# Block products of 256 columns: moving operand and result gone through in pieces of four columns, even pieces first

## The chip, the cores and the metric

The kernel runs on one core of one Trainium2 chip. The metric is device time in microseconds (us), the median of the runs of one program. Profiles are of one execution each. PE is TensorE's matmul, PEld its weight load, DVE VectorE, ACT ScalarE, POOL GpSimd, SP SyncE.

## What is computed

One decoder layer on 512 tokens and 16 learned meta tokens, width 2048, feed-forward width 5632, all in float32:

```python
n = rmsnorm(h, g_mix); p = n @ w_in                       # q, k, v | b, c, u
o_attn = stick_breaking_attention(rmsnorm(q), rmsnorm(k), v)   # 8 heads of 128
o_conv = b * causal_dwconv3(c * u)                        # 1024 channels
h = h + concat(rmsnorm(o_attn), rmsnorm(o_conv)) @ w_out
n2 = rmsnorm(h, g_ffn)
h = h + (silu(n2 @ w_gate) * (n2 @ w_up)) @ w_down
return h[:, N_META:]
```

## The kernel before

Activations are kept transposed: features on the 128 partitions, tokens as columns. A matmul takes a 128x128 tile of a weight matrix as the operand that is loaded into the array (LDWEIGHTS) and up to 512 token columns as the moving operand, and adds its result up in a bank of PSUM.

Every float32 operand is split into two float32r tiles, hi and lo: ACT casts (`split_quad`, L203), DVE subtracts (L206). A product of two such operands is three matmuls into the same bank: hi by hi, hi by lo, lo by hi. Each of them has its own weight load, so there are as many LDWEIGHTS as MATMULs.

The larger products go in pairs of output tiles. `pair_product` splits weights, activations and result into 2x2 blocks and forms them with seven block products where eight would be plain (weight sums `t1`, `t2`, `t3` are made by DVE, sums of activations once ahead of time). The token dimension is thus cut in halves of T2 = 256 columns. The seven block products go to three PSUM banks `y`, `z` and `x`; between them ACT copies partial results to `sides` (`read_out`, L912) and DVE combines them with later ones. After the last, ACT copies `x` out (L1267), and PE goes on with the next pair.

`block_product` does one block product: for each of n weight tiles along the contraction it issues the three matmuls of L887, L890 and L891, `act(part, k)` giving the hi or lo columns of tile k. It is used in three places:

- the convolution part (`conv_pair` with blocks of N = 258 columns, `gate_pair` with 256), whose operands are the `n` tiles and the packed `mixed` tiles;
- gate and up projections of the feed-forward part, operands `f` (44 pairs, 7 blocks, 8 tiles);
- the down projection, operands `ring` and `first` (chunks of 4, 6, 6 and 6 tiles).

Where a weight piece holds two output tiles, `ps` is 512 columns wide and is gone through in two halves of 256.

Where operands lie in SBUF is partly set by hand. `slots` puts the feed-forward operands four columns into their tile and adds a tail, and `pad` fills pools:

```python
        c = 2 * m * n * T2
        t = pool.tile([P, 4 + c + tail], dt, name=name, **kw)
        t = t[:, 4 : 4 + c].rearrange("p (s a k t) -> p s a k t", s=m, a=2, k=n)
```

The seven blocks of the convolution part come from tiles of two kinds. `raw_block` and `last_block` are columns of an `n` tile, `last_block` N = 258 columns further on than `raw_block(0, 0)`; the `mixed` blocks lie packed, 258 columns apart. `gate_pair` starts two columns further into each (`a` = 2) and takes 256:

```python
        return [
            raw_block(0, 0, a, n),
            *(mixed_block(t, a, n) for t in mixed),
            last_block(a, n),
            raw_block(1, 0, a, n),
            raw_block(1, 1, a, n),
        ]
```

The order of instructions on each engine comes from the program order and the priorities of the framework's scheduler; `keep_in_program_order` and `issue_after` pin single ones. SP's queue loads weights (`sw_in`), POOL's queue moves activations and results.

Of the kernel before, what the change touches and what calls it, by code (L numbers as in the profile page):

```python
# [26 lines left out]
T2 = SEQ // 2  # L27
# [6 lines left out]
def hybrid_layer(ctx: ExitStack, tc: tile.TileContext, xT, w_in, w_out, w_gu, w_down, vecs, out):  # L34
# [269 lines left out]
    def next_w():  # L304
        ahead = max(min(n_first, used[0] + 6), used[0] + 1 + S_AHEAD)
        if used[0] < n_first:
            ahead = min(ahead, n_first + 1)
        while len(split_w) < min(len(pieces), ahead):
            if n_first < len(split_w) <= n_first + S_AHEAD:
                with tc.issue_after(read_q0[3].ins):  # L310
                    prepare()
            else:
                prepare()
        used[0] += 1
        return split_w[used[0] - 1]
# [6 lines left out]
    def tick():  # L322
        for w in waiting:
            w[0] -= 1
        while any(w[0] <= 0 for w in waiting):
            w = next(w for w in waiting if w[0] <= 0)
            waiting.remove(w)
            w[1]()
# [156 lines left out]
    def host(m, name):  # L485
        return mpool.tile([P, 8 * N + (48 if m == 0 else 0)], F32R, tag=f"m{m}", name=name)
# [373 lines left out]
    def wide_product(parts, acts):  # L860
        hi, lo = next_w()
        for ps, a, b in parts:
            for n, (k, ah, al) in enumerate(acts):
# [4 lines left out]
                if b == SEQ:  # L868
                    tick()

    def block_product(ps, act, start):

        hi, lo = next_w()
        i = pieces[used[0] - 1][1]
        m = max(1, ps.shape[-1] // T2)
        cols = ps.shape[-1] // m  # L880
        n = pairs[i][0] // m
        for j in range(m):
            p, skip = ps[:, j * cols : (j + 1) * cols], m > 1 or not start
            for k in range(n):
                kk = slice((j * n + k) * P, (j * n + k + 1) * P)
                ah, al = act(0, k), act(1, k)
                opening = pe.matmul(p, hi[:, kk], ah, start=start and j == k == 0, stop=False, skip_group_check=skip)  # L887
                if j == k == 0:
                    tc.keep_in_program_order(opening)
                pe.matmul(p, hi[:, kk], al, start=False, stop=False, skip_group_check=skip)  # L890
                pe.matmul(p, lo[:, kk], ah, start=False, stop=k == n - 1, skip_group_check=skip)  # L891
# [8 lines left out]
    def pair_product(acts, cols, out2, side, fifth=None, hook=None):  # L900
# [16 lines left out]
        if first:  # L917
            block_product(y, acts[5], True)
            go_between()
        block_product(x, acts[0], True)  # L920
        read_out(p1, x)
        go_between()
        if hook:
            hook(1)
        block_product(z, acts[1], True)
        go_between()
        read_out(p5, z)
# [67 lines left out]
    for m in range(2):  # L995
        t = host(m, f"oa{m}")[:, : 4 * SEQ].rearrange("p (h a b) -> p h a b", h=2, a=2)
# [65 lines left out]
    for i, j in enumerate(OUT_TILES):  # L1062
# [36 lines left out]
        ps = ps_out[i]  # L1099
        half, k = divmod(j, 8)  # L1100
# [313 lines left out]
```

## Time and profile before

| what | us |
|---|---|
| median of 2 runs | 2027.59 (2027.51 to 2027.67) |
| span of the profiled execution | 2025.8 |
| attention part and its projections, up to the first block product | about 370 |
| convolution part and output projection, up to | 764 |
| feed-forward part | 764 to 2025.8 |

In rows of matmuls the form `128x256 f32` is the result's partitions and columns; `x<-f,sw_split` names the bank, the moving operand and the weights. A row of groups has count, busy time in us and mean duration in ns, then the idle time before. A row of windows has the stretch, its length, and busy time and number of instructions of each engine, then the granted clock, the share of the DMA engines and GB/s. A row of the timeline has start and duration in us.

### The profile page before, as it was taken

The numbers are of one execution on the slowest core, as the hardware profiler recorded it, in microseconds if no ns is written. First come the engines' busy times: TensorE is split into PE (matmuls) and PEld (weight loads), VectorE is DVE, ScalarE is ACT, GpSimd is POOL, SyncE is SP. The second block draws the span as 40 slices with busy tenths as digits, with TensorE's granted clock in tenths as the row PEclk, the third lists the DMA queues.
The fourth block names the chain that finished last, engine by engine and source line by source line (L and its number), as shares of the span: only waits on it lengthen the run. The fifth ranks groups of instructions, "written<-read, shape, count | busy, mean of one in ns | idle before, by whom it ended". The sixth has DMA issues, their size and how long they took to land.

```text
span 2025.8 us, 39704 instructions
## 1 busy us (share of the span) xinstructions
PE 2019.7 (100%) x16158; PEld 1961.8 (97%) x16158; DVE 1723.3 (85%) x2199; ACT 1077.9 (53%) x1559; POOL 337.3 (17%) x507
## 2 busy tenths in 40 slices
PE   9999999999999999999999999999999999999999
PEld 8999999999998889999999999999999999999999
DVE  7877777698877778999988988988988978888888
ACT  7876676444454445555555555555555544444443
POOL 0111111200014440111110110110110243131211
PEclk9999999999999999999999999999999999999999
DMA  6333343833255555556554554554554999797864
GB/s 222 116 135 115 125 136 136 282 105 110 99 198 179 165 161 194 171 153 186 173 160 148 167 164 149 164 166 151 162 166 151 290 339 352 170 318 193 222 149 91
DMA packets 156664, 356.31 MB, mean 176 GB/s; under 512 B 13696, under 2 KB 68224, under 8 KB 155712
## 3 DMA queue, kind: packets, MB, share of 16 engines
q1 hardware_dynamic: 72640, 216.73, 32.2%
q0 software_dynamic: 83696, 136.99, 25.0%
q8 instruction: 127, 2.08, 0.4%
q14 instruction: 57, 0.47, 0.1%
q10 hardware_dynamic: 144, 0.04, 0.0%
HBM read 275.78 MB, written 77.92 MB: 175 GB/s over the span
## 4 chain that ended last, share of the span: by engine, by line
PE 99%; DMA 0%; DVE 0%; SPq 0%; ACT 0%; issue 0%
PE x L887 14%; PE x L891 14%; PE x L890 14%; PE z L887 7%; PE z L890 7%; PE z L891 7%; PE y L891 3%; PE y L887 3%; PE y L890 3%; PE pk L342 3%; PE pv L342 3%; PE pq L342 3%; PE pv L340 2%; PE pk L340 2%; PE pq L340 1%; PE pb L342 1%
## 5 line engine op out<-in xcount | busy, mean ns | idle before, releaser
L203 ACT CAST sw_split<-sw_in 128x1024 fp32r<-128x1024 f32 (+3 forms) x671 | 662.4, 989 | 708.7 <-PE x L890 174.2
L206 DVE TENSOR_TENSOR sw_split<-sw_in,sw_split 128x1024 fp32r<-128x1024 f32 (+3 forms) x671 | 775.5, 1156 | 140.4 <-ACT sw_split L203 133.0
L887 PE MATMUL x<-f,sw_split 128*128 128x256 f32 x1408 | 387.5, 275 | 0.1
L891 PE MATMUL x<-f,sw_split 128*128 128x256 f32 x1408 | 387.2, 275 | 0.0
L890 PE MATMUL x<-f,sw_split 128*128 128x256 f32 x1408 | 387.2, 275 | 0.0
L887 PEld LDWEIGHTS x<-f,sw_split 128*128 128x128 f32 x1408 | 264.3, 188 | 0.7 <-DVE u L937 0.5
L890 PEld LDWEIGHTS x<-f,sw_split 128*128 128x128 f32 x1408 | 264.3, 188 | 0.0
L891 PEld LDWEIGHTS x<-f,sw_split 128*128 128x128 f32 x1408 | 264.3, 188 | 0.0
L1206 POOL DMA_DIRECT2D fd<-s x147 | 103.7, 921 | 708.0 <-DVE s L353 632.1
L887 PE MATMUL z<-f,sw_split 128*128 128x256 f32 x704 | 193.6, 275 | 0.0
L890 PE MATMUL z<-f,sw_split 128*128 128x256 f32 x704 | 193.6, 275 | 0.0
L891 PE MATMUL z<-f,sw_split 128*128 128x256 f32 x704 | 193.6, 275 | 0.0
L216 DVE TENSOR_TENSOR sw_in<-sw_in 128x1024 f32<-128x1024 f32 (+1 forms) x164 | 187.7, 1145 | 5.4 <-DMA sw_in<-w_in 0.8
L887 PE MATMUL x<-ring,sw_split 128*128 128x256 f32 x608 | 167.2, 275 | 0.0
L890 PE MATMUL x<-ring,sw_split 128*128 128x256 f32 x608 | 167.2, 275 | 0.0
L891 PE MATMUL x<-ring,sw_split 128*128 128x256 f32 x608 | 167.2, 275 | 0.0
L890 PEld LDWEIGHTS z<-f,sw_split 128*128 128x128 f32 x704 | 132.2, 188 | 0.0
L891 PEld LDWEIGHTS z<-f,sw_split 128*128 128x128 f32 x704 | 132.2, 188 | 0.0
L887 PEld LDWEIGHTS z<-f,sw_split 128*128 128x128 f32 x704 | 132.2, 188 | 0.0
L887 PEld LDWEIGHTS x<-ring,sw_split 128*128 128x128 f32 x608 | 114.1, 188 | 0.0
L891 PEld LDWEIGHTS x<-ring,sw_split 128*128 128x128 f32 x608 | 114.1, 188 | 0.0
L890 PEld LDWEIGHTS x<-ring,sw_split 128*128 128x128 f32 x608 | 114.1, 188 | 0.0
(701 smaller groups left out, 5276.9 us busy)
## 6 DMA issues: line engine op xcount, KB each, us to landing
sw_in<-w_gu SPq DMA_DIRECT2D x176, 512.0 KB, 3.8
sw_in<-w_in SPq DMA_DIRECT2D x90, 512.0 KB, 3.3
fd<-s POOLq DMA_DIRECT2D x147, 256.0 KB, 5.1
sw_in<-w_down SPq DMA_DIRECT2D x96, 384.0 KB, 4.2
ring<-fd POOLq DMA_DIRECT2D x42, 768.0 KB, 17.6
sw_in<-w_out SPq DMA_DIRECT2D x32, 512.0 KB, 3.3
out_T<-d POOLq DMA_DIRECT2D x54, 256.0 KB, 4.6
mix_dram<-st_x POOLq DMA_DIRECT2D x16, 516.0 KB, 4.1
```

The costliest lines, as they stand in the source:

```text
L203: cast[0] = sc.copy(hi, src)
L206: latest[0] = ve.tensor_tensor(lo, src, hi.bitcast(F32), ALU.subtract)
L216: return ve.tensor_tensor(sums[name], a, b, ALU.add)
L340: pe.matmul(ps, wh, ah[:, a:b], start=k + i == 0, stop=False)
L342: pe.matmul(ps, w, x[:, a:b], start=False, stop=k + i == last and x is (al if used[0] <= n_first else ah))
L887: opening = pe.matmul(p, hi[:, kk], ah, start=start and j == k == 0, stop=False, skip_group_check=skip)
L890: pe.matmul(p, hi[:, kk], al, start=False, stop=False, skip_group_check=skip)
L891: pe.matmul(p, lo[:, kk], ah, start=False, stop=k == n - 1, skip_group_check=skip)
L1206: gp.dma_start(fd[c][s][:, :, k], t[:, :, i])
```

## The change

A helper `order` rearranges a view of 256 columns: the columns are taken as 32 groups of 8, each group as two pieces of 4, and the dimension of the pieces is put first. An access through this view goes through the first pieces of all groups (columns 0 to 3, 8 to 11, 16 to 19 and so on) and then through the second pieces (4 to 7, 12 to 15 and so on). `block_product` applies it to the moving operand and to the result, so that each column's sum still lands in its own place. Views of other widths, the blocks of 258 columns among them, stay as they are. Weights are loaded as before.

```diff
+    def order(t):
+        return t.rearrange("p (m b i) -> p b m i", b=2, i=4) if t.shape[-1] == T2 else t
+
     def block_product(ps, act, start):
...
         for j in range(m):
-            p, skip = ps[:, j * cols : (j + 1) * cols], m > 1 or not start
+            p, skip = order(ps[:, j * cols : (j + 1) * cols]), m > 1 or not start
             for k in range(n):
                 kk = slice((j * n + k) * P, (j * n + k + 1) * P)
-                ah, al = act(0, k), act(1, k)
+                ah, al = (order(act(i, k)) for i in range(2))
```

On TensorE, in the feed-forward part, where the block product into bank `x` ends and that into `z` begins, the program before has these rows (line, operation, result and operands, size of the result):

```order
L890 MATMUL x_14131<-f_6536,sw_split 128x256
L891 MATMUL x_14131<-f_6536,sw_split 128x256
L887 MATMUL z_14130<-f_6537,sw_split 128x256
L890 MATMUL z_14130<-f_6537,sw_split 128x256
L891 MATMUL z_14130<-f_6537,sw_split 128x256
```

The changed program has these at the same place:

```order
L893 MATMUL x_14131<-f_6536,sw_split 128x2x32x4
L894 MATMUL x_14131<-f_6536,sw_split 128x2x32x4
L890 MATMUL z_14130<-f_6537,sw_split 128x2x32x4
L893 MATMUL z_14130<-f_6537,sw_split 128x2x32x4
L894 MATMUL z_14130<-f_6537,sw_split 128x2x32x4
```

The rows have new line numbers and the stepped shape, 2 by 32 by 4; none has moved. 11,592 matmuls have the new shape. On the other engines the instructions and their order are the same too, with one addition on ScalarE: 31 of the 44 copies of `x` (L1267 before, L1270 now) wait for VectorE as well. At one of them the program before has these rows, with the semaphores that each waits for (a CAST splits weights, ACTIVATE is the gate's SiLU):

```order
L203 CAST sw_split<-sw_in 128x1024 [waits DMAHW3_49,DVE_49,PE_49]
L203 CAST sw_split<-sw_in 128x1024 [waits DVE_49,PE_49]
L1267 COPY g_10695<-x_10699 128x256 [waits PE_49]
L203 CAST sw_split<-sw_in 128x1024 [waits DVE_49,Activation_49]
L1222 ACTIVATE g_10695<-g_10695 128x512 [waits DVE_49]
```

In the changed program they read:

```order
L203 CAST sw_split<-sw_in 128x1024 [waits DMAHW3_49,DVE_49,PE_49]
L203 CAST sw_split<-sw_in 128x1024 [waits DVE_49,PE_49]
L1270 COPY g_10695<-x_10699 128x256 [waits DVE_49,PE_49]
L203 CAST sw_split<-sw_in 128x1024 [waits DVE_49,Activation_49]
L1225 ACTIVATE g_10695<-g_10695 128x512 [waits DVE_49]
```

The count on VectorE that the copy now waits for is that of the subtraction that read `x` (`out2[1]` in `pair_product`) ahead of the last block product into it.

## The prediction

> **What bounds the kernel now.** I read the page first: its span, its share of busy time and the chain that ended last. The third row is the clock that TensorE was granted, in tenths.
>
> ```profile
> span 2025.8 us, 39704 instructions
> PE 2019.7 (100%) x16158; PEld 1961.8 (97%) x16158; DVE 1723.3 (85%) x2199; ACT 1077.9 (53%) x1559; POOL 337.3 (17%) x507
> PEclk9999999999999999999999999999999999999999
> PE 99%; DMA 0%; DVE 0%; SPq 0%; ACT 0%; issue 0%
> ```
>
> TensorE is busy for all of the span and 99% of the chain is matmuls. Nothing else is ever waited for at length. The kernel's time is therefore the number of matmuls times the spacing of their starts, and a change in that spacing goes to the end one for one. The median of the runs, 2027.59 us, lies 1.8 us above this span; I carry that 1.8 us as fixed.
>
> A "busy" matmul overlaps the next, so its duration isn't its cost. The spacing is read from counts. Next are a stretch of the feed-forward part with the columns PE, weight load, VectorE and ScalarE, and below it one of the three matmul lines alone from the start of that part to the end.
>
> ```profile
> 1200.00:1500.00 300.00, 300.00 (x2649) 300.00 (x2649) 268.11 (x299) 157.86 (x207) 35.98 (x51) 1.00 0.52 159
> ...
> 764.00:2025.80 1261.80, 1016.67 (x3696) 693.77 (x3696) 1.00 0.65 190
> ```
>
> 300 us hold 2649 matmuls, 113.3 ns each. L887 runs 3696 times, and L890 and L891 each as often (three matmuls per weight tile), so 11,088 matmuls of 256 columns fill 1261.8 us: 113.8 ns each with all gaps in it. This is 62% of the kernel, and there is no idle time in it that the change could uncover.
>
> The question is thus what one matmul of this shape costs, and the trace holds an answer that the count alone hides: equal shapes are not equally fast. These are starts from the timeline, in a gate product of the convolution part: first and twenty-first of a run of matmuls from the `n` tiles, and then first and last of 24 from other `n` tiles.
>
> ```profile
> 458.51 0.29 PE L887 MATMUL x<-n,sw_split 128*128 128x256 f32 x1
> ...
> 461.05 0.29 PE L891 MATMUL x<-n,sw_split 128*128 128x256 f32 x1
> ...
> 464.05 0.28 PE L887 MATMUL x<-n,sw_split 128*128 128x256 f32 x1
> ...
> 466.81 0.28 PE L891 MATMUL x<-n,sw_split 128*128 128x256 f32 x1
> ```
>
> The first run has 20 steps from 458.51 (there are 21 matmuls in it) in 2.54 us: 127.0 ns. The second has 23 steps in 2.76 us: 120.0 ns. With the 113.3 ns of the feed-forward part these are three levels, about 6.7 ns apart, for the same shape, engine and clock. What differs is where the operands lie: in tiles of one layout, the first run's block (`last_block`) begins 258 columns behind the second's (`raw_block`), which is 8 bytes more than 1024; and the code puts the feed-forward operands four columns into their tile (`slots`), with tails that keep this place equal from tile to tile. I read this as the moving operand's reads meeting those of the weight load, which goes on beside every matmul (97% busy in the first fence). That is a reading of the levels; the trace doesn't show the memory itself.
>
> **The change, part by part.** The edit changes in which order a matmul's 256 columns are read and written. All 11,592 matmuls of 256 columns in the block products have it: the 11,088 above and 504 gate matmuls of the convolution part. The order of instructions stays on every engine, so nothing is cost there, and no transfer is issued elsewhere.
>
> 31 copies on ScalarE get one more wait, on VectorE. It is for the read of the same bank that stands before the copy's own matmuls, and TensorE waits for that read already before it writes the bank again.
>
> ```profile
> L1267 ACT COPY g<-x x44: 358/373/377, 784.4 to 1603.3; 128x256 f32<-128x256 f32 x44
>   PE x L891: 70.8, 42
> ```
>
> The copy is released by TensorE (42 of 44 times), later than VectorE's read. Behind it ScalarE holds weight casts and the gate's activation. I cost it at nothing: ScalarE is busy for 157.86 of 300 us above, and one more 373 ns each, were that cover gone, would be 31 x 0.37 = 11 us of ScalarE's time, not TensorE's.
>
> What is left is the spacing of 11,592 matmuls. No matmul of this trace steps through its columns, so the price of that has to be bounded by rows of unstepped matmuls. In the rows by shape the mean duration stands in for the spacing, since both grow together (275 with 113.3, 284 or 285 with the mix of 120 and 127).
>
> ```profile
> L887 PE MATMUL x<-f,sw_split 128*128 128x256 f32 x1408 | 387.5, 275 | 0.1
> ...
> L890 PE MATMUL x<-n,sw_split 128*128 128x256 f32 x72 | 20.5, 285 | 0.0
> ...
> L887 PE MATMUL z<-mixed,sw_split 128*128 128x256 f32 x48 | 13.5, 282 | 0.0
> L891 PE MATMUL z<-mixed,sw_split 128*128 128x256 f32 x48 | 13.4, 280 | 0.0
> L890 PE MATMUL z<-mixed,sw_split 128*128 128x256 f32 x48 | 13.4, 279 | 0.0
> ```
>
> The nearest rows are those of `mixed`. Its blocks lie packed, 258 columns apart, so that the place of the moving operand against the weights shifts from one matmul to the next and no fixed relation holds. With the new order the same is true inside each matmul: the reads run through every second piece at twice the pace in address, then through the others, while the weights are read as before. The place that the feed-forward tiles were given stops being a place. Their mean is (282 + 280 + 279) / 3 = 280.3 ns, 5.3 ns over 275.
>
> The sum: 11,088 x 5.3 ns = 58.8 us. The 504 gate matmuls pace like this already and get nothing (one level for all, 504 x 6.7 ns = 3.4 us, is their end on both sides). 2025.8 + 58.8 + 1.8 = 2086.4, so 2086 us. The ends among unstepped rows are 279 (+4 ns, 44 us, 2072) and 285 (+10 ns, 111 us, 2138).
>
> The price may also be below nothing. The levels are steps of 6.7 ns, and 113.3 needn't be the lowest: one step further down for all is 11,592 x 6.7 = 77.7 us. VectorE, busy for 268.11 of 300 us, would then be at 95% and wouldn't yet bound.
>
> [...]
>
> **The rivals.**
>
> *Unchanged.* The 113.3 ns isn't a meeting of reads, but the rate at which such columns come at all, and a piece of four is as good as a row. For it: within the feed-forward part the spacing never varies, whatever the other engines do (113.3 over 300 us in which VectorE and ScalarE write all the time); and the 512-column matmuls of the next fence last 391 - 275 = 116 ns longer for 256 more columns, nearly the same rate. Against it: the levels of the `n` tiles. Time: 2027.6.
>
> *Lower level.* The new order keeps the moving reads away from the weight reads, and the spacing falls below 113.3. For it: the levels show that what is lost depends on places alone, and pieces of four columns are 16 bytes, twice the shift that parted the two `n` runs. Against it: no feed-forward row is lower, and only half of the meeting streams is reordered. Time: one full step, 2027.6 - 77.7 = 1950; anything between is open. This is the one on the other side. It decides if a matmul comes at less than 109.8 ns: 3.5 ns x 11,592 = 40.6 us, 2% of the time.
>
> *A price per piece.* Each of 64 pieces is fetched or added up as an access of its own. For it: the run shifted by 8 bytes, where a piece of four would straddle, is the dearest. Against it: pieces stay whole, and no row shows a price for a break. It decides above +10 ns. At two levels up, 13.4 ns x 11,592 = 155 us, it gives 2183; its far end is that a matmul of half-used rows costs as one of 512:
>
> ```profile
> L342 PE MATMUL pq<-n,sw_split 128*128 128x512 f32 x256 | 79.4, 391 | 0.0
> ```
>
> That is 116 ns x 11,592 = 1345 us, 3372. I take the near end.
>
> [...]
>
> That the change doesn't do what it says is out: the program's rows have the stepped shape on all 11,592 matmuls.
>
> **How the numbers follow.** Forecast, the fixed place lost: 0.33, of which 0.05 ends below +2%. Unchanged: 0.23. Lower level: 0.28, of which a little over half (0.15) reaches the 3.5 ns that make 2%, because the levels come as whole steps. Price per piece: 0.16. So faster by over 2% 0.15, within 2% 0.23 + 0.13 + 0.05 = 0.41, slower by over 2% 0.28 + 0.16 = 0.44; 2% is about what a measurement of this kernel tells from no change. The first three cases have 0.84. Their range goes from the full step, 1950 (with its rounding 1948), to the dearest unstepped row, 2138 (2140), and leaves out the price per piece. Both signs are in it; the forecast's own range is 2060 to 2140.
>
> **What would show it.** The count in 300 us of the feed-forward part, 2649 now: about 2530 with the forecast (118.6 ns), the same if unchanged, over 2730 below 109.8 ns, under 2430 above 123.3. The gate products should hardly move by the forecast, and by 13 ns or more by a price per piece. The clock row must stay at 9, or the spacing says nothing. The forecast is wrong if the feed-forward rows stay at one exact level, and its reading of the levels too if matmuls with a shifted and an unshifted place come out alike and still cost more.

## The result, and the profile after

| | us |
|---|---|
| before, median | 2027.59 (2027.51 to 2027.67) |
| after, median of 2 runs | 2086.96 (2086.9 to 2087.02) |
| ratio, 95% interval | 1.0293 (1.0263 to 1.0323) |
| span of the profiled execution after | 2085.2 |

The kernel became 2.9% slower, 59.4 us. The forecast was 2086. That it came so close is luck in good part: two of its terms were wrong by over 20 us each, in opposite directions.

The page of the kernel after: span, busy shares, the granted clock in tenths, and the shares of the chain that ended last.

```profile
span 2085.2 us, 39735 instructions
PE 2080.1 (100%) x16158; PEld 2017.8 (97%) x16158; DVE 1727.6 (83%) x2199; ACT 1075.3 (52%) x1559; POOL 338.1 (16%) x507
PEclk9999999999999999999999999999999999999999
PE 100%; DVE 0%; issue 0%
```

The clock is the same, the number of matmuls is the same, and the chain is matmuls from end to end. So the 59.4 us are matmuls that start further apart. The view by windows (length, then busy time and count of PE, weight load, VectorE, ScalarE and GpSimd) tells where: first the feed-forward stretch after, then a stretch with gate products after.

```profile
1200.00:1500.00 300.00, 300.00 (x2574) 300.00 (x2573) 261.12 (x292) 152.15 (x201) 36.02 (x51) 1.00 0.50 152
440.00:468.00 28.00, 28.00 (x173) 26.42 (x173) 18.55 (x21) 8.79 (x11) 0.00 (x0) 1.00 0.23 78
```

The same 28 us of the kernel before:

```profile
440.00:468.00 28.00, 28.00 (x236) 28.00 (x235) 25.08 (x30) 12.16 (x15) 0.00 (x0) 1.00 0.34 117
```

In the feed-forward part 2649 matmuls became 2574: 116.6 ns each in place of 113.3. In the stretch with gate products 236 became 173: 161.8 ns in place of 118.6. The dear place is the one that was forecast to stay as it is. The groups by shape (count, busy us, mean ns of one, idle time before) show which matmuls it is:

```profile
L890 PE MATMUL x<-f,sw_split 128*128 128x256 f32 x1408 | 393.7, 280 | 0.0
...
L893 PE MATMUL x<-n,sw_split 128*128 128x256 f32 x72 | 23.3, 323 | 0.0
...
L890 PE MATMUL z<-mixed,sw_split 128*128 128x256 f32 x48 | 19.7, 411 | 0.0
L894 PE MATMUL z<-mixed,sw_split 128*128 128x256 f32 x48 | 18.8, 392 | 0.0
L893 PE MATMUL z<-mixed,sw_split 128*128 128x256 f32 x48 | 14.5, 301 | 0.0
...
L894 PE MATMUL y<-n,sw_split 128*128 128x256 f32 x24 | 6.7, 281 | 0.0
```

`mixed` went from some 280 ns to 411 at L890, `x<-n` to a mean of 323, while `y<-n` kept 281. The mean of `x<-n` mixes two kinds, which the timeline (start, duration) parts: first and last of the 24 matmuls of a run from `last_block`, then the second and the last of the run from `raw_block` behind it.

```profile
463.11 0.41 PE L890 MATMUL x<-n,sw_split 128*128 128x256 f32 x1
...
468.37 0.41 PE L894 MATMUL x<-n,sw_split 128*128 128x256 f32 x1
...
468.73 0.28 PE L893 MATMUL y<-n,sw_split 128*128 128x256 f32 x1
...
471.31 0.28 PE L894 MATMUL y<-n,sw_split 128*128 128x256 f32 x1
```

23 steps in 5.26 us are 228.7 ns, where this run had 127.0 before. 22 steps in 2.58 us are 117.3 ns, where it was 120.0. The first run begins 8 bytes off a multiple of 16, so that each piece of four columns lies half in one line of 16 bytes and half in the next (a line here is four columns from a multiple of 16 bytes on); the second run is aligned.

Added up by operand and place from all starts in the two traces (the difference from each matmul to the next), the 59.4 us split so:

| matmuls | count | ns before | ns after | us |
|---|---|---|---|---|
| feed-forward | 11,088 | 113.4 | 116.7 | +36.7 |
| `n`, 8 bytes off 16 (`last_block`) | 72 | 126.5 | 228.3 | +7.3 |
| `mixed`, in threes of which two are 8 bytes off | 216 | 118.1 | 193.3 | +16.2 |
| `n`, aligned | 216 | 119.9 | 117.9 | -0.4 |
| sum | | | | +59.8 |

The 116.7 ns are a mean of two: behind the first of the 44 pairs of gate and up products, the starts of the kernel after lie in turn 119.2 and 114.2 ns apart, where before they are near 113.4 at every place of a block.

The added wait on ScalarE did what was expected of it. The view of line L1270 (durations least, median, most; then what ended the idle time before it) has:

```profile
L1270 ACT COPY g<-x x44: 368/374/375, 807.7 to 1650.3; 128x256 f32<-128x256 f32 x44
L1270 ACTq EVENT_SEMAPHORE  x31: 17/17/17, 1059.4 to 1647.4; - x31
...
  PE x L894: 74.6, 42
```

31 waits of 17 ns on its queue, and the copy is still released by TensorE 42 of 44 times.

### The profile page after: what moved, and what is told of

Same layout as the page of the kernel before. It is cut to its first block, busy times and chain, and to the rows that moved or that the text cites. A ratio compares the mean times of both kernels' runs of the same rounds, so it can differ in the third digit from the quotient of the medians.

```text
span 2085.2 us, 39735 instructions
## 1 busy us (share of the span) xinstructions
PE 2080.1 (100%) x16158; PEld 2017.8 (97%) x16158; DVE 1727.6 (83%) x2199; ACT 1075.3 (52%) x1559; POOL 338.1 (16%) x507
## 4 chain that ended last, share of the span: by engine, by line
PE 100%; DVE 0%; issue 0%
PE x L890 14%; PE x L894 14%; PE x L893 14%; PE z L890 7%; PE z L894 7%; PE z L893 7%; PE y L890 3%; PE y L893 3%; PE y L894 3%; PE pk L342 3%; PE pv L342 3%; PE pq L342 3%; PE pv L340 2%; PE pk L340 1%; PE pq L340 1%; PE pb L342 1%
## 5 line engine op out<-in xcount | busy, mean ns | idle before, releaser
L890 PE MATMUL x<-f,sw_split 128*128 128x256 f32 x1408 | 393.7, 280 | 0.0
L893 PE MATMUL x<-f,sw_split 128*128 128x256 f32 x1408 | 393.6, 280 | 0.0
L894 PE MATMUL x<-f,sw_split 128*128 128x256 f32 x1408 | 393.5, 279 | 0.0
L890 PEld LDWEIGHTS x<-f,sw_split 128*128 128x128 f32 x1408 | 264.5, 188 | 0.5 <-DVE u L940 0.5
L893 PEld LDWEIGHTS x<-f,sw_split 128*128 128x128 f32 x1408 | 264.5, 188 | 0.0
L894 PEld LDWEIGHTS x<-f,sw_split 128*128 128x128 f32 x1408 | 264.5, 188 | 0.0
L890 PE MATMUL z<-f,sw_split 128*128 128x256 f32 x704 | 196.8, 280 | 0.0
L893 PE MATMUL z<-f,sw_split 128*128 128x256 f32 x704 | 196.8, 280 | 0.0
L894 PE MATMUL z<-f,sw_split 128*128 128x256 f32 x704 | 196.7, 279 | 0.0
L890 PE MATMUL x<-ring,sw_split 128*128 128x256 f32 x608 | 169.9, 280 | 0.0
L893 PE MATMUL x<-ring,sw_split 128*128 128x256 f32 x608 | 169.9, 280 | 0.0
L894 PE MATMUL x<-ring,sw_split 128*128 128x256 f32 x608 | 169.9, 279 | 0.0
L893 PEld LDWEIGHTS z<-f,sw_split 128*128 128x128 f32 x704 | 132.3, 188 | 0.0
L894 PEld LDWEIGHTS z<-f,sw_split 128*128 128x128 f32 x704 | 132.3, 188 | 0.0
L890 PEld LDWEIGHTS z<-f,sw_split 128*128 128x128 f32 x704 | 132.2, 188 | 0.0
L893 PEld LDWEIGHTS x<-ring,sw_split 128*128 128x128 f32 x608 | 114.2, 188 | 0.0
L894 PEld LDWEIGHTS x<-ring,sw_split 128*128 128x128 f32 x608 | 114.2, 188 | 0.0
L890 PEld LDWEIGHTS x<-ring,sw_split 128*128 128x128 f32 x608 | 114.2, 188 | 0.0
```

## The experiments

Per-kind spacings below are means of the time from one matmul's start to the next in the feed-forward part, worked out from the starts in the trace and grouped by the line that issued the matmul. Each kernel in which orders, sides, places or starts take turns ran once, so that its matmuls are compared with each other inside one execution, at a granted clock of 1.00 in all but the one with moved starts. A profile row beside them shows the duration, which moves with the spacing but isn't equal to it: in the run of the sides 276 ns beside 113.5, 280 beside 117.8.

### Which part costs: feed-forward alone, gate products alone

Two kernels with the new order in one part only; the other part is as before.

```diff
-        return t.rearrange("p (m b i) -> p b m i", b=2, i=4) if t.shape[-1] == T2 else t
+        return t.rearrange("p (m b i) -> p b m i", b=2, i=4) if t.shape[-1] == T2 and pieces[used[0] - 1][1] >= CONV else t
```

The second kernel has `< CONV` there.

> The new order in the feed-forward part alone; the 504 gate matmuls as before. If the two parts simply add (in the profile of the change the 11,088 feed-forward matmuls start 116.7 ns apart against 113.3, about 36.8 us, and the gate stretches take about 23 us more), this gives 2027.6 + 37 = 2064 us and feed-forward matmuls at 116.7 ns. By the recorded forecast (58.8 us from the feed-forward part, nothing from the gates) it would give 2086.

> The new order in the 504 gate matmuls alone. If the parts add, 2027.6 + 23 = 2050.5 us, with matmuls near 228 ns apart where the moving operand starts 8 bytes off a multiple of 16, and the feed-forward part at 113.3 ns. By the recorded forecast the gates cost nothing: 2027.6.

Measured: feed-forward alone 2064.05 us against 2027.62 before, ratio 1.018 (1.0165 to 1.0195); gate products alone 2050.47 us, ratio 1.0113 (1.0096 to 1.013). The same feed-forward window, of the first kernel and then of the second:

```profile
1200.00:1500.00 300.00, 300.00 (x2573) 300.00 (x2573) 262.89 (x294) 152.36 (x202) 38.98 (x56) 1.00 0.53 155
```

```profile
1200.00:1500.00 300.00, 300.00 (x2649) 300.00 (x2648) 268.99 (x300) 157.47 (x206) 38.10 (x54) 1.00 0.54 159
```

36.4 + 22.9 = 59.3 us: the two parts add up to the whole change, and neither disturbs the other. 504 matmuls cost 22.9 us, 11,088 cost 36.4.

### Which side costs: moving operand or result

The feed-forward products take turns by `i % 4`: plain, both sides stepped, the moving operand alone, the result alone. In the last two the columns of a result come to lie in other places.

```diff
+        kind = i % 4 if i >= CONV else 0
...
+                elif kind == 2:
+                    opening = pe.matmul(p, hi[:, kk], order(ah), start=start and j == k == 0, stop=False, skip_group_check=skip)
+                elif kind == 3:
+                    opening = pe.matmul(order(p), hi[:, kk], ah, start=start and j == k == 0, stop=False, skip_group_check=skip)
```

> Feed-forward pairs in turn: plain order; new order on both sides; new order of the moving operand alone; new order of the result alone (in the last two the result's columns land in other places than the reference's, the amount of work is the same). Theory meeting (the moving reads meet the weight reads): plain 113.3, both 116.7, moving alone 116.7, result alone 113.3 ns between starts. Rival result (stepping through the bank costs): moving alone 113.3, result alone 116.7. If each side has a share, both lie between.

| | plain | both | moving alone | result alone |
|---|---|---|---|---|
| ns | 113.5 | 117.8 | 117.8 | 113.8 |

The first matmul of the three, by groups, in the order moving alone, both, result alone, plain:

```profile
L891 PE MATMUL x<-f,sw_split 128*128 128x256 f32 x352 | 98.9, 281 | 0.0
L889 PE MATMUL x<-f,sw_split 128*128 128x256 f32 x352 | 98.7, 280 | 0.0
...
L893 PE MATMUL x<-f,sw_split 128*128 128x256 f32 x352 | 97.3, 276 | 0.0
...
L887 PE MATMUL x<-f,sw_split 128*128 128x256 f32 x352 | 97.1, 276 | 0.0
```

The whole price is in the reads of the moving operand: 117.8 ns with it alone, as with both. How the result is written into its bank costs at most 0.3 ns in this order (113.8 against 113.5). The new order takes 117.8 ns here and 116.7 in the changed kernel, in which every pair has it; why isn't shown.

### What in the order costs: the break, the piece or the step

Eight orders take turns, with `b` pieces of `i` columns in each group; the pieces of one turn lie `b` times `i` columns apart. (2, 4) is the change.

```diff
-    def order(t):
-        return t.rearrange("p (m b i) -> p b m i", b=2, i=4) if t.shape[-1] == T2 else t
+    def order(t, b, i):
+        return t.rearrange("p (m b i) -> p b m i", b=b, i=i) if t.shape[-1] == T2 else t
...
+        kind = i % 8 if i >= CONV else 0
```

> Feed-forward pairs in turn, both sides in orders of (pieces in turn, columns of a piece): plain, (2,4), (2,2), (4,2), (2,8), (2,16), (4,4), (16,4). Theory meeting, with reads by lines of 16 bytes (4 columns): (2,2) and (4,2) touch every line twice and come near 2 x 113 = 227 ns; (2,4), (4,4) and (16,4) touch each once and differ only by how they meet the weight reads, 113 to 120; (2,8) and (2,16) 113 to 120. Rival price per break of the order: (2,4) has 64 pieces and costs 3.3 ns, so (2,2) with 128 pieces 6.7 (120 ns), (2,8) 1.7 (115), (2,16) 0.8 (114), and (4,4) and (16,4) 3.3 like (2,4).

Another eight in the same manner:

> Orders (pieces in turn, columns of a piece) plain, (4,4), (8,4), (32,4), (4,8), (8,8), (4,16), (2,64) in feed-forward pairs in turn. All touch each 16-byte line once. Theory meeting with a memory that is spread over lines in a short cycle: the step in address decides. (4,4) again 113.3; steps of 128 bytes and more, (8,4) and (32,4), hit the same part of the memory over and over and are dearer, between 120 and 140 like (16,4) with 134.7; long pieces, (4,16) and (2,64), lose their place in part, 113 to 119. Rival jump price (a fixed price for each jump in address): it would follow the count of jumps, (8,4) and (32,4) like (4,4).

| order (b, i) | plain | (2, 4) | (4, 4) | (8, 4) | (16, 4) | (32, 4) | (2, 2) | (4, 2) |
|---|---|---|---|---|---|---|---|---|
| ns | 113.3 to 113.6 | 117.8 | 113.4, 113.5 | 120.5 | 134.7 | 126.7 | 228.9 | 233.3 |

| order (b, i) | (2, 8) | (4, 8) | (8, 8) | (2, 16) | (4, 16) | (2, 64) |
|---|---|---|---|---|---|---|
| ns | 117.5 | 115.6 | 129.5 | 118.6 | 117.9 | 113.6 |

Rows of the first of the two kernels: (2, 2), (2, 8), (16, 4), (2, 4), plain, (4, 4).

```profile
L891 PE MATMUL x<-f,sw_split 128*128 128x256 f32 x192 | 78.2, 408 | 0.0
...
L895 PE MATMUL x<-f,sw_split 128*128 128x256 f32 x192 | 54.0, 281 | 0.0
...
L901 PE MATMUL x<-f,sw_split 128*128 128x256 f32 x160 | 48.0, 300 | 0.0
...
L889 PE MATMUL x<-f,sw_split 128*128 128x256 f32 x160 | 44.8, 280 | 0.0
...
L887 PE MATMUL x<-f,sw_split 128*128 128x256 f32 x160 | 44.0, 275 | 0.0
...
L899 PE MATMUL x<-f,sw_split 128*128 128x256 f32 x160 | 43.8, 274 | 0.0
```

A price per break is out. (4, 4) has the same 64 pieces as (2, 4) and is free (113.4 ns); (2, 16) has a quarter of them and costs as much (118.6 against 117.8). Pieces of two columns, half a line of 16 bytes, double the time (228.9 and 233.3). Above that, the price goes with the step between the pieces and with their length, and not in an even manner: a step of 16 columns is free at (4, 4) and costs 4 ns at (2, 8), and one of 64 columns takes 134.7, 129.5 and 117.9 ns with pieces of 4, 8 and 16. That a memory spread over lines in a short cycle is met at the same part again was a reading; the runs show the times alone. No order came below 113.3. Each order was run at one place of its operands and weights only; what it takes at others isn't shown.

### Whether the place decides: weights read from other places

Plain order in the one kernel, the new order in the other. In both the feed-forward products take turns by `i % 16`: the weights are read 0 to 15 lines of four columns further on, so that a product uses other columns of its weights. A tile with no room behind it is read one tile further back, shifted by as much. Moving operand and result stay where they are.

```diff
+    def shifted(w, kk, lines):
+        at = kk.start + 4 * lines
+        return w[:, at : at + P] if at + P <= w.shape[-1] else w[:, at - P : at]
...
+        kind = i % 16 if i >= CONV else 0
```

> Feed-forward pairs in turn, plain order, with the weights of each matmul read 0 to 15 lines of 16 bytes further on in the weight tile than they should (so other columns of weights are used, as many as before). Theory meeting: the spacing depends on the distance between moving and weight addresses, 113.3 ns at 0, and up to 120 ns at others, with a pattern that repeats; the levels 113.3 and 120 of the convolution part's tiles should both turn up. Rival rate (113.3 is how fast columns come): 113.3 at all sixteen.

> The same sixteen places with the new order on both sides. Theory meeting, as the forecast had it (no fixed place is left): 116.7 ns at 0 and close to it, within 1.5 ns, at all sixteen. Rival: the new order too has places, and the change only moved the relation: then some of the sixteen come at 113.3 or less and others at 120 or more.

| lines | 0 | 1 | 2 | 3 | 4 | 5 | 6 | 7 |
|---|---|---|---|---|---|---|---|---|
| plain, ns | 113.6 | 119.9 | 120.0 | 118.4 | 118.4 | 118.4 | 116.7 | 118.3 |
| new order, ns | 119.2 | 117.8 | 117.6 | 117.8 | 117.8 | 117.8 | 117.6 | 117.8 |

| lines | 8 | 9 | 10 | 11 | 12 | 13 | 14 | 15 |
|---|---|---|---|---|---|---|---|---|
| plain, ns | 117.2 | 120.0 | 119.2 | 113.5 | 119.3 | 117.4 | 115.1 | 120.0 |
| new order, ns | 120.0 | 120.0 | 117.5 | 117.8 | 117.8 | 117.8 | 116.7 | 117.4 |

Groups of the plain kernel at 0, 1 and 11 lines, and then of the one with the new order at the same:

```profile
L891 PE MATMUL x<-f,sw_split 128*128 128x256 f32 x96 | 26.5, 276 | 0.0
L893 PE MATMUL x<-f,sw_split 128*128 128x256 f32 x96 | 27.2, 283 | 0.0
...
L913 PE MATMUL x<-f,sw_split 128*128 128x256 f32 x96 | 26.4, 275 | 0.0
```

```profile
L891 PE MATMUL x<-f,sw_split 128*128 128x256 f32 x96 | 27.4, 285 | 0.0
L893 PE MATMUL x<-f,sw_split 128*128 128x256 f32 x96 | 26.7, 278 | 0.0
...
L913 PE MATMUL x<-f,sw_split 128*128 128x256 f32 x96 | 27.1, 282 | 0.0
```

Between the columns of a table the edit changes the address of the weights alone, and the plain order runs from 113.5 to 120.0 ns. Two of its places, 0 and 11, have the low level throughout, and 14 lines has it in the gate and up products (113.4 ns; 118.7 in the down products). The kernel before stands on one of them. The new order has 116.7 to 120.0 wherever it is, and its low level is nowhere; but its spread of 3.3 ns is more than the 1.5 that was expected, so it isn't wholly free of places either. One point doesn't fit: at 0 lines it took 119.2 here and 116.7 in the changed kernel, where the code gives that matmul the same addresses. So its own addresses don't settle a matmul's spacing alone; what else does stays open.

### What doubles the gate products: the start of the moving operand

In the feed-forward products all matmuls but the first of each block product have 248 columns, so that their start can be moved; eight columns of a result lack those terms. By `i % 8`, the start is at column 0, 2 or 4 of moving operand and result, or differs between the two, in plain and in the new order.

```diff
+                elif kind == 5:
+                    opening = pe.matmul(order(p[:, 2 : 250]), hi[:, kk], order(ah[:, 2 : 250]), start=start and j == k == 0, stop=False, skip_group_check=skip)
...
+                elif kind == 7:
+                    opening = pe.matmul(order(p[:, 2 : 250]), hi[:, kk], order(ah[:, 0 : 248]), start=start and j == k == 0, stop=False, skip_group_check=skip)
```

> Feed-forward pairs in turn, 248 of the 256 columns in all matmuls but the first of each block (8 columns get one matmul's share only). Start of moving and result at column 0, 2, 4 of 256, plain; moving at 2 with result at 0, plain; the same starts in the new order; and moving at 0 with result at 2, new order. Theory lines (a piece that straddles 16 bytes is read in two lines): plain 0 and 4 near 113.3 x 248/256 = 110, plain 2 up to 120, new order 0 and 4 near 113, new order 2 near 228 x 248/256 = 221, and moving at 0 with result at 2 near 113. Rival result: moving at 0 with result at 2 comes near 221 too.

In this kernel TensorE was idle for 86.5 us before the first matmuls of block products into `x` from `f` (L887), 86.4 of it until ScalarE's copies out of a bank to `sides` (L955) ended, and the granted clock was 0.974, so medians of the spacing are given here.

| start | 0 | 2 | 4 | one 0, other 2 |
|---|---|---|---|---|
| plain, ns | 114 | 120 | 115 | 120 (moving 2, result 0) |
| new order, ns | 116 | 225 | 114 | 116 (moving 0, result 2) |

The groups of the new order at start 2, at 0, and with the result alone at 2:

```profile
L899 PE MATMUL x<-f,sw_split 128*128 128x248 f32 x168 | 68.2, 406 | 0.0
...
L897 PE MATMUL x<-f,sw_split 128*128 128x248 f32 x168 | 49.3, 293 | 0.0
...
L903 PE MATMUL x<-f,sw_split 128*128 128x248 f32 x140 | 41.0, 293 | 0.0
```

Two columns, 8 bytes, off a multiple of 16 double a stepped read: 225 ns against 116 and 114. A plain one is 6 ns dearer by its median (120 against 114), which is weaker evidence: at start 0 the plain spacings lie at 109 to 112 and again at 115 to 118, so that 114 is between them, and 110 was expected. It is the start of the moving operand that counts (plain, 120 ns with it alone at 2); that of the result does nothing (new order, 116 ns with it alone at 2, as at 0). This is the 228 ns of `last_block`, and what made `mixed` dear.

### Is the place of the feed-forward tiles what was lost

Both kernels have the feed-forward operands four columns lower in their tiles, the first in the plain order throughout, the second with the new order in the feed-forward part.

```diff
-        t = t[:, 4 : 4 + c].rearrange("p (s a k t) -> p s a k t", s=m, a=2, k=n)
+        t = t[:, :c].rearrange("p (s a k t) -> p s a k t", s=m, a=2, k=n)
```

> The kernel before, plain order, with the feed-forward operands one line of 16 bytes earlier (column 0 of their tile in place of column 4). Theory meeting: the distance to the weights is that of the place 1 in the run of sixteen places, 119.9 ns, so 2027.6 + 11,088 x 6.5 ns = 2100 us. Rival: the place run measured the shifted weights and not the distance; then 113.3 ns and 2027.6 us.

> The new order in the feed-forward part with the operands moved by the same 16 bytes. Theory meeting: the new order keeps no place, so it costs the same as unmoved, 116.7 to 117.8 ns, 2064 to 2077 us, and is then faster than the plain order at this place (2100). Rival: the new order loses a fixed amount over plain at any place: 119.9 + 3.3 ns, 2137 us.

Measured: plain 2101.04 us against 2027.51 before, ratio 1.0362 (1.0346 to 1.0377); new order 2064.19, ratio 1.018 (1.0163 to 1.0197). The window, of the plain kernel and then of the other:

```profile
1200.00:1500.00 300.00, 300.00 (x2502) 300.00 (x2501) 256.81 (x284) 149.04 (x194) 34.64 (x49) 1.00 0.51 149
```

```profile
1200.00:1500.00 300.00, 300.00 (x2574) 300.00 (x2573) 262.91 (x293) 152.44 (x202) 39.18 (x56) 1.00 0.53 155
```

Sixteen bytes cost the plain order 73.5 us: 119.9 ns, the same mean as with the weights one line further on. The new order doesn't notice this move: 2064.19 here, 2064.05 at the old place. It is 1.8% slower than the plain order at the right place and faster than it at the wrong one (2064 against 2101).

### An order that loses nothing

The feed-forward part in four pieces of four columns, (4, 4), which was free above.

```diff
-        return t.rearrange("p (m b i) -> p b m i", b=2, i=4) if t.shape[-1] == T2 else t
+        return t.rearrange("p (m b i) -> p b m i", b=4, i=4) if t.shape[-1] == T2 and pieces[used[0] - 1][1] >= CONV else t
```

> The whole feed-forward part in pieces of four columns, but every fourth piece in turn (4,4) in place of every second; gates plain. Theory meeting: as in the run of orders, 113.3 to 113.5 ns, so 2027.6 to 2030 us: it is the step that loses the place, not that the row is broken into pieces. Rival price per break: 64 pieces as in the change, 116.7 ns, 2064 us.

Measured 2027.43 us against 2027.51, ratio 0.9999 (0.9989 to 1.0008). The ratio is that of nine executions; a tenth took 2098.64 us, and why isn't shown.

```profile
1200.00:1500.00 300.00, 300.00 (x2650) 300.00 (x2648) 268.20 (x300) 158.26 (x207) 36.07 (x52) 1.00 0.54 159
```

2650 matmuls in 300 us, as before. Sixty-four pieces as such cost nothing over a whole kernel, and they gain nothing. No version here beats the kernel before.

## Why the prediction was right, and where it was not

**What bounds the kernel.** Right. The chain is matmuls before and after, and 3.3 ns on 11,088 of them are 36.7 us of the end's time, one for one. VectorE at 261.12 of 300 us never came to bound.

**The added waits on ScalarE.** Right: 17 ns each, behind a copy that waits for TensorE anyway.

**"The place that the feed-forward tiles were given stops being a place."** Right in the main, as far as times show. The kernel before stands on a level that the plain order has throughout at 2 of 16 places of the weights; moved by 16 bytes it takes 2101.04. The stepped order takes 2064 at either place. It isn't the breaking up as such that gives the place up, since (4, 4) keeps 113.4, and not all places are gone, since 8 and 9 lines take 120.0 against 116.7 at 14. That the weight loads are the other party was a reading of the levels, and shifting the weights alone now shows that their address matters (113.5 to 120.0 ns in the plain order). Which reads meet, and where, no trace here shows.

**"The levels come as whole steps".** Wrong. The plain order takes 116.7, 117.2 and 118.3 ns at some places, between 113.3 and 120, and the new order alternates between 119.2 and 114.2. The run that gave 127.0 was also misread as one of 21 matmuls: it has 24, from 458.14 us, and all of them average 126.5.

**The term "11,088 x 5.3 ns = 58.8 us".** Mis-sized: it measured 3.3 ns, 36.7 us. The step that failed is the stand-in. The rise in mean duration from 275 to the 280.3 of `mixed` was taken for the rise in spacing. The duration after is indeed 280, but the spacing rose by 3.3 and not by 5.3; `mixed` itself had a spacing of 118.1 before, 4.7 above the feed-forward part. So 0.6 ns of the error is duration taken for spacing, and 1.4 ns is that packed blocks are not stepped reads. The count in 300 us came at 2574, where 2530 was forecast.

**"The 504 gate matmuls pace like this already and get nothing".** Wrong: 22.9 us with the change in them alone. The prediction knew that `last_block` begins 8 bytes off and that a piece of four would straddle there, but it used this only as an argument for the rival, and drew no term for those matmuls. The 72 of `n` went to 228.3 ns. A three of `mixed` sums to 580; by its starts the matmuls at L890, L893 and L894 take some 230, 138 and 212, so the two that straddle are the dear ones. These 22.9 us happen to make up for the 22.1 that the first term had too much; with that term at its measured size and nothing for the gates, the forecast would have been 2064.

**The rival of a price per piece.** Dead as it was put: (4, 4) has 64 pieces and costs nothing (113.4 ns). What is real in it goes by lines of 16 bytes: pieces of two columns, which don't fill one, took 228.9 ns, and pieces of four that straddle two took 225 ns from the start at column 2, against 114 from column 4. Longer stepped pieces weren't run at such a start. On the result's side pieces of four cost next to nothing (113.8 against 113.5 ns); shorter ones on that side alone weren't run.

**The rivals "unchanged" and "lower level".** Both fell. The rate of 113.3 ns is not that of the plain order (2 of 16 places have it throughout), and neither 13 stepped orders nor 16 places show anything below it. (4, 4) shows how near "unchanged" was: with twice the step, the change would have cost nothing in the feed-forward part (2027.43 us).

**The tests the prediction named.** The gate products moved by more than 13 ns, which it had put down to a price per piece, and they did so in 216 of 504 alone. Its last test, that its reading of the levels is wrong if shifted and unshifted places come out alike and dearer, was badly chosen: that is what a lost place looks like, and it did happen (2064.19 and 2064.05). The reading had to be tested on the plain order, where moving the operands, or the weights, changes the level.

## What to carry to other kernels

Where TensorE bounds, read the spacing of starts by operand and by place, not the duration and not one mean: equal shapes here took from 113 to 233 ns at a full clock. Before a moving operand is stepped, look at its first byte and its pieces: here pieces of two columns, half a line of 16 bytes, took 228.9 ns, and pieces of four in a block that begins 8 bytes off 228.3 where the plain order took 126.5, a loss even if such matmuls are few (216 of 11,592 made 39% of it). A place in memory that a kernel has been given is worth checking by moving it 16 bytes (73.5 us here), and a new order of the reads can give it up, as (2, 4) did here (2064.05 us), or keep it, as (4, 4) did (2027.43).

## What was not expected of the hardware

- The spacing of a plain matmul of 256 columns depends on the address of its weights, in lines of 16 bytes: 113.5 to 120.0 ns over 16 places, in an edit that shifts the weights alone.
- Writing into a result's bank in the new order was free: 113.8 against 113.5 ns.
- The price of a stepped read isn't even in its step: in pieces of four columns 117.8, 113.5, 120.5, 134.7 and 126.7 ns for 2, 4, 8, 16 and 32 pieces. Why, these runs don't tell, nor why 113.3 ns is the least.
